# Recurrent unit's end: fifth gate's gelu behind the last root, six early half outputs of the projection in four passes

## The chip, the core and the metric

The kernel runs on one core of one Trainium2 chip. The core has a matrix engine (TensorE, PE in the profile; PEld is its weight load), a vector engine (VectorE, DVE), a scalar engine that evaluates functions from loaded tables (ScalarE, ACT), GpSimd (POOL) and a queue engine that issues transfers (SyncE, SP). Each works through its own instructions in a fixed order; semaphores tie them together. Data lies in SBUF, 128 partitions wide, and matrix products go to PSUM, which has eight banks. The metric is the device time of one execution in microseconds (us).

## The reference, cut to what matters

One inference step of two layers over 640 tokens (512 latent, 128 context) of width 1024. Layer 0 is attention and a gated feed-forward network (FFN). Layer 1, where the change lies, is a recurrent unit and another FFN:

```python
gate, xr = split(xm @ w_in)                       # two halves, 1024 wide each
xc = centred_depthwise_conv(xr)                   # width 4
r, i = sigmoid(xc @ w_a + b_a), sigmoid(xc @ w_i + b_i)   # 8 blocks of 128, per direction
a = exp(log_a);  log_a = -8 * r * softplus(-lam)
b = sqrt(-expm1(2 * log_a)) * (i * xc)            # "the root"
h_t = a_t * h_{t-1} + b_t                         # one scan per direction
y = (h_forward + h_backward) * gelu(gate)
x = x + g1 * (y @ w_out)                          # "the projection"
x = x + g2 * swiglu(modulate(rms_norm(x)))        # the FFN
```

## The kernel before, in words

All activations are kept with features on the partitions: 1024 features are KT = 8 tiles of 128, numbered 0 to 7, and the 640 tokens run along the free side. Products are in full precision by splitting: each operand is a rounded `hi` and a remainder `lo`, and a tile of a product is three matmuls, hi*hi, hi*lo and lo*hi (`some`, L227 to L229). A weight block `unit` (L163) is loaded to `raw` (three buffers), rounded to `hi` (in the recurrent unit by a transfer on POOL's queue, L178, elsewhere by ACT, L180) and its remainder is made by DVE (L182). `whi` and `wlo` have three buffers each; in the last stage every second block takes a second set, `whx` and `wlx`.

**The recurrent unit** is a pipeline over the eight feature tiles, in the loop at L1458. At step t the program writes down: block t's convolution and gate matmuls with their Tanh (`lru_a`), tile t+1's product xr (`lru_xr`), block t-1's Exp, Tanh and root (`lru_b`, the root is the Sqrt at L1305), block t-2's two scans (`lru_c`, L1316, and their sum, L1323 and L1324), the gelu gate of tile t-2 (`lru_gate`) and its output (`lru_d`): y times gelu (L1328, DVE), then the split of y into `yhi` (L1333, ACT) and `ylo` (L1335, DVE). Gates 1 to 7 are thus written at steps 3 to 9.

Gelu, Exp with Tanh, and Sqrt lie in different tables of ACT. `turn` (L1266) chains the functions in the order of the program and writes a table load (L1270) where the table changes. In the steady state a step has three loads: Exp, Sqrt and Gelu. A gate has two halves in PSUM, 384 and 256 tokens: the first is copied out at once (L1343), the second stays in its bank until gelu reads it there (L1346), and then gelu runs over the copied part.

PSUM in this stage: three banks `mm` (for xr, the gates and, later, the projection), one `at`, and two pairs `gp` for the gate matmuls of `lru_a`. When the last of these is read, the four banks become `mx` (three) and `mc` (one) of the next stage.

**The projection** (`project_halves`, L1028) makes 8 outputs in two halves of 320 tokens, CH = (0, 320), (320, 640). Of the half outputs a few are `early`: they are begun over the input tiles 0 to 5 of y while the recurrent unit is still finishing, in `mm` and `mx` banks in turn, and closed over tiles 6 and 7 in a second pass, with four matmuls on constants in between (`keep`, L206) that hold the clock up. There are five: both halves of outputs 0 and 1, and the first half of output 2. Then follow the first halves of outputs 3 to 7, and then the second halves of outputs 2 to 7 (DEH = 6). `out` adds the result to x (`residual`, L597) and stores it; x itself is loaded back from DRAM first (`load_x`, L1355), into memory that the recurrent unit's buffers held. `stat` sums the squares (L550, L553), and the normalisation of the first token half (`first_half`: L994, L995, L1333, L1335) is written between the second halves, two tiles at a time. The FFN's first products (`plain`, L1154) read it.

The order on each engine is not the program's: a planner simulates a timeline with its own costs when the program is built, takes the instructions in the order of the program where several are ready, and places others earlier where an engine would wait. So matmuls of the projection come between those of the last gates. `issue_after` and `pin` force an order where they stand.

Of the kernel before, what the change touches and what calls it, by code (L numbers as in the profile page):

```python
# [17 lines left out]
KT = D // P  # L18
# [3 lines left out]
CH = ((0, 320), (320, 640))  # L22
# [20 lines left out]
DEH = 6  # L43
# [82 lines left out]
class _Step:  # L126
# [901 lines left out]
    def project_halves(self, w, hi, lo, gk, key, xd):  # L1028
        def out(f, t0, t1, ps):
            self.residual(f, t0, t1, ps, G, True)  # L1030
            self.nc.sync.dma_start(xd[f * P:f * P + P, t0:t1], self.x[:, f, t0:t1])
        G = self.need(self.gcols, gk)
        us = [self.unit(w[f], "m") for f in range(3)]
        early = [(f, t0, t1) for f in range(3) for c, (t0, t1) in enumerate(CH) if c == 0 or f < KT - DEH]
        pss = [(self.ps("mx") if j % 2 else self.pg(False))[:, 0:HT] for j in range(len(early))]
        for ks in (range(KT - 2), range(KT - 2, KT)):
            if ks[0]:
                self.keep(self.ps("at"), 4)
            for (f, t0, t1), ps in zip(early, pss):
                self.some(us[f], hi, lo, t0, t1, ps, ks)  # L1040
                if ks[0]:
                    out(f, t0, t1, ps)
        for f in range(3, KT):
            us.append(self.unit(w[f], "mx"[f % 2]))
            out(f, *CH[0], self.chunk(us[f], hi, lo, *CH[0]))
        self.rt = self.t([P, NTOK], F32, "r", 2)
        for c, (t0, t1) in enumerate(CH):
            for f in range(KT - DEH, KT) if c else ():
                out(f, t0, t1, self.chunk(us[f], hi, lo, t0, t1))
                j = f - KT + DEH  # L1050
                for k in range(max(0, 2 * j - 2), 2 * j) if f < KT - 1 else ():
                    self.first_half(k, key)
            self.stat(t0, t1)
            self.nc.scalar.copy(self.rt[:, t0:t1], self.r[0][:, 0:t1 - t0])
# [302 lines left out]
    def run(self):  # L1357
# [82 lines left out]
        yhi = self.big()  # L1440
        ylo = self.big()
        with self.phase("lru", at=1) as lp:
            A, B, C, G = {}, {}, {}, {}
            self.table, self.last_act = AF.Gelu_apprx_tanh, None
            self.xrs = [self.t([P, 648], F32, f"xr{j}", 1, lp) for j in range(2)]
            for xr in self.xrs:
                for a, b in ((0, 2), (514, 517), (645, 648)):
                    nc.gpsimd.memset(xr[:, a:b], 0.0)

            def gate(g, after=None):  # L1450
                G[g], halves = self.lru_gate(g, xhi, xlo, lp, after)
                return halves
            x0, g0, x1 = self.lru_xr(0, xhi, xlo), gate(0, self.sq), self.lru_xr(1, xhi, xlo, self.dg)
            x0[0](pins={3: self.at})
            g0[0](pins={0: self.rr})
            for step in (x1[0], x0[1], g0[1]):
                step()
            for t in range(KT + 2):  # L1458
                if t < KT:
                    A[t] = self.lru_a(t, lp)  # L1460
                if t + 1 < KT:
                    for step in self.lru_xr(t + 1, xhi, xlo) if t else x1[1:]:
                        step()
                if 0 < t <= KT:
                    B[t - 1] = self.lru_b(t - 1, *A.pop(t - 1))
                if t > 1:
                    C[t - 2] = self.lru_c(t - 2, *B.pop(t - 2))
                if t > 2:
                    for step in gate(t - 2):
                        step()  # L1470
                if t > 1:
                    self.lru_d(t - 2, C.pop(t - 2), G.pop(t - 2), yhi, ylo)
            nc.gpsimd.dma_start(o["nh"], self.st)
        x1, x2 = self.big(n=NTOK + 2), self.big(n=NTOK + 2)
        self.new_x(self.ctx)
# [32 lines left out]
```

## Time and profile before

| | |
|---|---|
| median of 3 runs | 1519.43 us (1516.95 to 1521.25) |
| the profiled execution | 1518.63 us, of which the span of instructions is 1516.9 us |
| granted clock of TensorE, mean | 0.996 of full speed |
| recurrent unit, projection | about 840 to 1020 us, then until about 1066 us |
| last root (L1305) starts | 1008.66 us |
| last remainder of y (L1335) ends | 1021.35 us |
| transfers in all | 196.65 MB, 130 GB/s |

The page gives the busy time of each engine; a busy PE is not PE at its peak. A row of a timeline is: start in us, duration in us, engine, line, operation, output<-input by the program's names, count, and in brackets the idle time of the engine before it and what ended it. A row of waits is: who waited for whom, us in total, times, the longest. Rows by stage give busy times with counts of instructions in brackets.

### The profile page before, as it was taken

To read this page: it belongs to the slowest core of one execution; us is meant where nothing else is said; L and a number is where in the kernel's file an instruction comes from. 1 tells how busy PE (TensorE), PEld (TensorE's weight loads), DVE (VectorE), ACT (ScalarE), POOL (GpSimd) and SP (SyncE) were. 2 spreads that over 40 slices of the span, in tenths; PEclk is the share of its full clock that TensorE was granted. 3 is DMA by queue.
4 is the path that set the end of the run, shared out by engine and by line. 5 is a ranking of instruction groups with operands and counts; after the bars stand their busy time and mean duration, and the time that the engine had idled before them with its cause. 6 is when DMAs were issued, how large, how long until landed. Compare 5 with 4: busy or idle time off the path is not lost. (4 is left out here: it accounts for less than half of the span.)

```text
span 1516.9 us, 26173 instructions
## 1 busy us (share of the span) xinstructions
PE 1490.0 (98%) x10397; PEld 1443.2 (95%) x10397; DVE 1063.5 (70%) x2005; ACT 702.6 (46%) x1270; POOL 260.6 (17%) x276
## 2 busy tenths in 40 slices
PE   8999999999999999999999999989999999999997
PEld 6999999899999999999999988889999999999997
DVE  5778998679999997434443768886975665566555
ACT  4676766654332123312321568884644342434243
POOL 0112132101111110000000014230332323222211
PEclk9999999999999999999999999999999999999999
DMA  9544665446566664222222544325242231323211
GB/s 376 175 142 159 187 190 168 118 141 193 180 182 196 206 197 132 62 84 84 65 69 87 153 133 128 105 68 198 70 152 84 70 112 56 104 64 98 70 57 70
DMA packets 72330, 196.65 MB, mean 130 GB/s; under 512 B 8048, under 2 KB 24592, under 8 KB 72080
## 3 DMA queue, kind: packets, MB, share of 16 engines
q1 hardware_dynamic: 57392, 142.32, 29.7%
q0 software_dynamic: 14240, 51.98, 11.3%
q8 instruction: 81, 1.33, 0.4%
q10 hardware_dynamic: 576, 0.68, 0.1%
q14 instruction: 41, 0.34, 0.1%
HBM read 179.48 MB, written 8.92 MB: 124 GB/s over the span
## 5 line engine op out<-in xcount | busy, mean ns | idle before, releaser
L227 PE MATMUL mm<-big,whi 128*128 128x320 f32 (+3 forms) x1233 | 385.4, 314 | 5.7 <-ACT gl L1346 3.0
L228 PE MATMUL mm<-big,whi 128*128 128x320 f32 (+3 forms) x1233 | 384.8, 312 | 4.9 <-DVE big L1335 4.7
L229 PE MATMUL mm<-big,wlo 128*128 128x320 f32 (+3 forms) x1233 | 383.5, 312 | 0.0
L227 PEld LDWEIGHTS mm<-big,whi 128*128 128x128 f32 x1233 | 233.7, 190 | 8.6 <-ACT gl L1346 3.5
L228 PEld LDWEIGHTS mm<-big,whi 128*128 128x128 f32 x1233 | 234.1, 190 | 6.9 <-DVE big L1335 5.3
L229 PEld LDWEIGHTS mm<-big,wlo 128*128 128x128 f32 x1233 | 233.6, 190 | 1.0
L256 DVE SCALAR_TENSOR_TENSOR mprod<-mraw,csb 128x1024 f32<-128x1024 f32 x160 | 195.6, 1222 | 11.9 <-DMA mraw<-in_wm 11.4
L597 DVE SCALAR_TENSOR_TENSOR x<-mm,G,x 128x320 f32<-128x320 f32 (+2 forms) x192 | 78.0, 435 | 81.8 <-PE mm L229 81.5
L180 ACT CAST whi<-raw 128x1024 fp32r<-128x1024 f32 (+1 forms) x71 | 73.9, 1041 | 112.5 <-PE mm L228 65.5
L182 DVE TENSOR_TENSOR wlo<-raw,whi 128x1024 fp32r<-128x1024 f32 (+1 forms) x87 | 105.8, 1216 | 27.4 <-ACT whi L180 11.4
L227 PE MATMUL mm<-big,whx 128*128 128x320 f32 (+3 forms) x348 | 108.3, 311 | 0.0
L229 PE MATMUL mm<-big,wlx 128*128 128x320 f32 (+3 forms) x348 | 108.0, 310 | 0.0
L228 PE MATMUL mm<-big,whx 128*128 128x320 f32 (+3 forms) x348 | 107.8, 310 | 0.0
L252 POOL DMA_DIRECT2D mraw<-in_wm x80 | 43.1, 539 | 359.0 <-DVE mprod L256 266.1
L227 PE MATMUL mx<-big,whi 128*128 128x320 f32 (+3 forms) x287 | 89.1, 311 | 0.0
L229 PE MATMUL mx<-big,wlo 128*128 128x320 f32 (+3 forms) x287 | 88.8, 310 | 0.0
L228 PE MATMUL mx<-big,whi 128*128 128x320 f32 (+3 forms) x287 | 88.6, 309 | 0.0
L180 ACT CAST whx<-raw 128x1024 fp32r<-128x1024 f32 (+1 forms) x40 | 41.1, 1030 | 86.7 <-PE mm L228 47.6
L227 PE MATMUL mx<-big,whx 128*128 128x320 f32 (+3 forms) x260 | 80.6, 310 | 0.0
L229 PE MATMUL mx<-big,wlx 128*128 128x320 f32 (+3 forms) x260 | 80.5, 310 | 0.0
L228 PE MATMUL mx<-big,whx 128*128 128x320 f32 (+3 forms) x260 | 80.3, 309 | 0.0
L1333 ACT CAST whi<-raw 128x1024 fp32r<-128x1024 f32 (+1 forms) x41 | 41.3, 1008 | 70.8 <-PE mm L228 44.8
(349 smaller groups left out, 3727.8 us busy)
## 6 DMA issues: line engine op xcount, KB each, us to landing
raw<-in_gu SPq DMA_DIRECT2D x88, 512.0 KB, 3.5
mraw<-in_wm POOLq DMA_DIRECT2D x80, 512.0 KB, 4.0
raw<-in_dn SPq DMA_DIRECT2D x24, 512.0 KB, 3.6
sw<-in_wm SPq DMA_DIRECT2D x16, 512.0 KB, 10.5
raw<-in_wqk SPq DMA_DIRECT2D x16, 512.0 KB, 4.6
raw<-in_wi SPq DMA_DIRECT2D x16, 512.0 KB, 3.5
whi<-in_wi POOLq DMA_DIRECT2D x16, 512.0 KB, 4.0
raw<-in_dn SPq DMA_DIRECT2D x16, 448.0 KB, 3.3
```

The source lines that it names most:

```text
L180: nc.scalar.copy(hi, raw)
L182: nc.vector.tensor_tensor(lo, raw, hi.bitcast(F32), ALU.subtract)
L227: nc.tensor.matmul(ps, hi[:, k], xhi[:, k, s], start=(k == 0), stop=False)
L228: nc.tensor.matmul(ps, hi[:, k], xlo[:, k, s], start=False, stop=False)
L229: self.done = nc.tensor.matmul(ps, lo[:, k], xhi[:, k, s], start=False, stop=(k == last)).ins
L252: nc.gpsimd.dma_start(w, self.i["wm"][l * 6 + j - 2, f])
L256: nc.vector.scalar_tensor_tensor(prod, w, 1.0, self.csb[:, s], ALU.mult, ALU.mult, accum_out=out[:, s, f:f + 1])
L597: self.nc.vector.scalar_tensor_tensor(xs, ps[:, a - t0:b - t0], G[:, s, f:f + 1], xs, ALU.mult, ALU.add)
L1333: self.nc.scalar.copy(hi, v)
```

## The change

In the recurrent unit step 7 writes no gate and no output. Step 8 writes, behind block 7's root and block 6's scans, gate 5 and its output, then gate 6 and its output. Step 9 writes gate 7 and its output as before. In the order of ACT's functions the gelu of gate 5 thus stands behind the last root, with those of gates 6 and 7.

In the projection six half outputs are early, both halves of outputs 0, 1 and 2, so the third `mx` bank is used as well. They are taken in four passes over y's tiles: 0 to 4, then 5, then 6, then 7, with the four constant matmuls ahead of the last pass, which also hands out the results. The loop of second halves begins at output 3.

```diff
-        early = [(f, t0, t1) for f in range(3) for c, (t0, t1) in enumerate(CH) if c == 0 or f < KT - DEH]
+        early = [(f, t0, t1) for f in range(3) for t0, t1 in CH]
         pss = [(self.ps("mx") if j % 2 else self.pg(False))[:, 0:HT] for j in range(len(early))]
-        for ks in (range(KT - 2), range(KT - 2, KT)):
-            if ks[0]:
+        for ks in (range(KT - 3), (KT - 3,), (KT - 2,), (KT - 1,)):
+            if ks[-1] == KT - 1:
                 self.keep(self.ps("at"), 4)
             for (f, t0, t1), ps in zip(early, pss):
                 self.some(us[f], hi, lo, t0, t1, ps, ks)
-                if ks[0]:
+                if ks[-1] == KT - 1:
                     out(f, t0, t1, ps)
...
         for c, (t0, t1) in enumerate(CH):
-            for f in range(KT - DEH, KT) if c else ():
+            for f in range(max(3, KT - DEH), KT) if c else ():
                 out(f, t0, t1, self.chunk(us[f], hi, lo, t0, t1))
...
                     C[t - 2] = self.lru_c(t - 2, *B.pop(t - 2))
-                if t > 2:
-                    for step in gate(t - 2):
+                for g in {KT - 1: (), KT: (KT - 3, KT - 2)}.get(t, (t - 2,)):
+                    for step in gate(g) if g > 0 else ():
                         step()
-                if t > 1:
-                    self.lru_d(t - 2, C.pop(t - 2), G.pop(t - 2), yhi, ylo)
+                    if g >= 0:
+                        self.lru_d(g, C.pop(g), G.pop(g), yhi, ylo)
```

## The prediction

> **What bounds the kernel now.** I read the page, the 5 us stages, PE's waits around the recurrent unit's end, then the timelines of PE, ACT and DVE from 960 to 1070 us. The page's first rows:
>
> ```profile
> span 1516.9 us, 26173 instructions
> PE 1490.0 (98%) x10397; PEld 1443.2 (95%) x10397; DVE 1063.5 (70%) x2005; ACT 702.6 (46%) x1270; POOL 260.6 (17%) x276
> ```
>
> TensorE (PE) sets the time, so an edit is worth the PE time that is lost where it acts. The rows of stages (columns: us, PE busy, PEld, DVE, ACT, POOL, granted clock, DMA share, GB/s) find such a place at the unit's end, and PE's waits there name two releasers:
>
> ```profile
> 1000.00:1010.00 10.00, 6.23 (x42) 5.46 (x40) 8.80 (x13) 9.88 (x13) 4.12 (x2) 1.00 0.18 53
> 1010.00:1013.00 3.00, 1.33 (x6) 1.31 (x6) 2.97 (x3) 2.72 (x5) 0.00 (x0) 0.50 0.00 0
> ```
>
> ```profile
> PE mm L228 <- DVE big L1335: 3.4, 1, 3.4
> PE mm L227 <- ACT gl L1346: 1.7, 1, 1.7
> ```
>
> ACT is busy 9.88 of 10 us, PE 6.23, and then the clock is at half. PE's timeline gives the price:
>
> ```profile
> 1002.02 0.31 PE L227 MATMUL mm<-big,whi 128*128 128x320 f32 x1
> ...
> 1008.87 0.42 PE L228 MATMUL mm<-big,whi 128*128 128x320 f32 x1 [3.37 <-DVE big L1335]
> ...
> 1009.72 0.31 PE L229 MATMUL mx<-big,wlo 128*128 128x320 f32 x1
> 1011.69 0.64 PE L227 MATMUL mm<-big,whi 128*128 128x320 f32 x1 [1.67 <-ACT gl L1346]
> ...
> 1016.65 0.35 PE L227 MATMUL mm<-big,whi 128*128 128x320 f32 x1
> ...
> 1019.37 1.05 PE L210 MATMUL at<-ident,ones 128*128 128x128 f32 x8
> 1020.18 0.39 PE L227 MATMUL mm<-big,whi 128*128 128x320 f32 x1
> ...
> 1024.72 0.31 PE L227 MATMUL mx<-big,whx 128*128 128x320 f32 x1
> ...
> 1039.00 0.31 PE L227 MATMUL mm<-big,whx 128*128 128x320 f32 x1
> ...
> 1042.54 0.31 PE L227 MATMUL mm<-big,whx 128*128 128x320 f32 x1
> ```
>
> A half output is eight input tiles of three matmuls: from 1039.00 to 1042.54, **3.54 us, or 0.443 a tile** ("fNcM" below is half M of output N). At half clock, from 1011.69 to 1016.65, six tiles took 4.96 us, 0.827 each: 2.30 lost. Of the five early halves, ten tiles in the mx banks lie before 1002.02; the other 30 need 13.29, and the four keep-warm matmuls 0.81 (1019.37 to 1020.18). They take from 1002.02 to 1024.72, 22.70 us. So 8.6 us are lost, and no edit here can win more. Counted to the work that the new order has done by then (f2c1 too), before ends at 1024.72 + 3.54 = 1028.26.
>
> **The change, part by part.** *Gelu 5 behind the last root.* ACT's order at the end:
>
> ```profile
> 998.85 1.28 ACT L1270 ACT_TABLE_LOAD   x1
> 1000.14 0.39 ACT L1346 ACTIVATE gl<-mm 128x256 f32<-128x256 f32 x1
> ...
> 1000.96 1.28 ACT L1270 ACT_TABLE_LOAD   x1
> 1002.26 0.93 ACT L1303 ACTIVATE lt<-lt,l_sm 128x643 f32<-128x643 f32 x1
> 1003.09 1.04 ACT L180 CAST whi<-raw 128x1024 fp32r<-128x1024 f32 x1
> 1004.03 0.72 ACT L1333 CAST big<-lt 128x640 fp32r<-128x640 f32 x1
> 1004.65 0.92 ACT L1304 ACTIVATE lt<-lt,l_sp 128x643 f32<-128x643 f32 x1
> ...
> 1008.66 1.28 ACT L1305 ACTIVATE lt<-lt 128x1286 f32<-128x1286 f32 x1
> 1009.96 1.28 ACT L1270 ACT_TABLE_LOAD   x1
> 1011.25 0.39 ACT L1346 ACTIVATE gl<-mm 128x256 f32<-128x256 f32 x1
> ...
> 1011.95 0.38 ACT L1346 ACTIVATE gl<-mm 128x256 f32<-128x256 f32 x1
> ```
>
> Root 6 ends just ahead of the load of 998.85. One table load now goes (1.29) and gelu 5's pair moves back (0.82): the first Exp of block 7 starts 2.12 earlier, where the load of 998.85 ends. The cast of y(5) at 1004.03 (0.62 to the next start) moves back too. So the last root starts at 1008.66 - 2.12 - 0.62 = 1005.92, 2.74 earlier; the three gelus follow a load, 0.70 apart, and free their mm banks at about 8.51 + 0.39 = **1008.9**, 1009.6 and 1010.3. The moved gate's weight transfers pass POOL's state copies and SP's loads in program order; they stay covered, since the last of them on POOL was issued some 40 us before:
>
> ```profile
> 970.25 0.53 POOL L178 DMA_DIRECT2D whi<-in_wi  x1 [8.70 <-PE mm L229]
> ```
>
> *The price of it.* Gate 5's second half keeps one of three mm banks until 1008.9 instead of 1000.5; gates 6 and 7 keep the others. So f0c0, f1c0 and f2c0, all in mm, cannot begin before 1008.9, where f0c0 had five tiles in from 1002.02. On DVE, y(5) = y*G now waits for gelu 5, and behind it stand y(6), the last scans, and y(7).
>
> *The sixth half* f2c1 takes the third mx bank, so three mx halves of five tiles can run without gelu: 15 tiles instead of 10 + 5, the same fill, if f2's weights are there. Those follow gate 7's second half (one of three whi buffers): cast at 1003.09, remainder by DVE:
>
> ```profile
> 1001.82 0.82 DVE L1328 TENSOR_TENSOR lt<-lt,gl 128x640 f32<-128x640 f32 x1
> 1002.55 1.28 DVE L1316 TENSOR_TENSOR_SCAN lt<-lt,cols,lt 128x512 f32<-128x512 f32 x1
> ...
> 1005.56 1.20 DVE L182 TENSOR_TENSOR wlo<-raw,whi 128x1024 fp32r<-128x1024 f32 x1
> ...
> 1009.97 1.50 DVE L1306 SCALAR_TENSOR_TENSOR lt<-lt,lt 128x1286 f32<-128x1286 f32 x1 [1.16 <-ACT lt L1305]
> ...
> 1012.92 0.82 DVE L1328 TENSOR_TENSOR lt<-lt,gl 128x640 f32<-128x640 f32 x1
> 1013.66 1.28 DVE L1316 TENSOR_TENSOR_SCAN lt<-lt,cols,lt 128x512 f32<-128x512 f32 x1
> ...
> 1018.90 0.83 DVE L1328 TENSOR_TENSOR lt<-lt,gl 128x640 f32<-128x640 f32 x1
> 1020.52 0.83 DVE L1335 TENSOR_TENSOR big<-lt,big 128x640 fp32r<-128x640 f32 x1 [0.79 <-ACT big L1333]
> ```
>
> y(5)'s product (0.73 to the next start) leaves the place ahead of the scans, so the remainder ends at 1005.56 + 1.20 - 0.73 = 1006.03. PE idles from 1002.02 to there, 4.0 us but for two matmuls; the third of f2c1's first tile waits, and all of PE behind it. Bounds: at full clock f2c1 is done at 1008.24 and hidden, PE goes on at 1008.95 with 33 tiles (14.62) and 0.81, and ends at 1024.38: **3.88 won**. At half clock, as before had it after waits of 3.37 and 1.67 us, for the same 4.96 us: f2c1 until 1010.16, one more slow tile (0.38), end at 1010.16 + 14.62 + 0.38 + 0.81 = 1025.97: **2.29 won**. I take this end, as it is nearest to the row that shows the clock fall.
>
> The rule that speaks against the change is in the Trainium skill, "TensorE: Matmul & The Clock Gate", Part 1 (The HAM clock gate): the clock halves after an idle window of about 3.4 us and returns after as long a busy one, the windows running freely. One gap of 4.0 us would by it be throttled more surely than waits of 3.37 and 1.67; the trace agrees so far that the matmuls between these two (1008.87 to 1009.72) still ran at full clock. With 3.4 us of half speed from 1006.03 the estimate by that page ends at 1025.3, 3.0 won.
>
> *Four passes.* Tile 5 is asked after 15 mm tiles, at 1008.95 + 6.65 = 1015.6 at the earliest. The last root ends at 1007.2; DVE's two products behind it take 2.95 (in before 1009.97 to 1012.92, ahead of y(6)), so at 0.74 each y(5) and y(6) are multiplied by 1011.7 and the last scans start there. y(7)'s product starts 5.24 behind the scans' start in before (1013.66 to 1018.90), now 0.74 more for y(5)'s remainder: at 1017.6, 1.3 earlier, and y(7)'s remainder ends 2.45 later, at 1020.1. PE asks for it at 1021.7 at the earliest (the end less six tiles): covered by 1.6; without that cover each us late costs one. If y(5)'s remainder lies ahead of that of y(6), between the scans and their sums, it is there by 1015.6 too: I cost it at nothing.
>
> *Outputs.* All six banks are now full when f3 starts, so it needs a residual add, and that needs x reloaded:
>
> ```profile
> 1019.88 2.18 SPq L1355 DMA_DIRECT2D x<-xd  x4
> DMA to landing us min/median/max: 3.9/5.9/8.5
> ```
>
> The reload follows y(7)'s product by 0.98: issue at 1018.6, landed 3.9 later at 1022.5, and the first banks are free about 1.2 later. f3 starts at 1024.4 to 1026.0: hidden, by 0.7 to 2.3; a reload that is later by more than that costs what is over.
>
> *One chunk less in the second half-loop* shortens what covers the normalisation of the first half:
>
> ```profile
> 1064.34 0.89 DVE L1335 TENSOR_TENSOR big<-x,big 128x320 fp32r<-128x320 f32 x2
> ...
> 1068.97 0.31 PE L1154 MATMUL mm<-big,whx 128*128 128x320 f32 x1
> ```
>
> From f7c0's end (1042.54) the last split took until 1065.23, 22.7; PE asked for it at 1068.97, 26.4 after. Now it asks 3.54 sooner, 22.9 after. Margin 0.2: I cost it at nothing.
>
> **Sum.** Profiled execution 1518.63 (span 1516.9 and 1.7 around it), less 2.29: 1516.34. It lies 0.80 under the median of 1519.43, so the median is forecast at **1517.1**, 0.15% under: within 0.3% (4.6 us), about what a measurement of this kernel can tell from no change.
>
> **Rivals.** *Full clock in the gap*: 3.88 won, median 1515.5. For it: the matmuls of 1008.87 ran full behind a gap; against: the 0.50 soon after.
>
> *The sixth half doesn't fill the gap*: a planner fixed PE's order; if it puts f2c1 behind f0c0, PE stands from 1002.02 to 1008.95, then 38 tiles (16.83), 0.81 and a half-clock loss of 2.30: 1028.89, 0.6 worse than before, median 1520.1. For it: the cast at 1003.09 sits in ACT's bound chain, and may slip behind the last root. Against: mx ran ahead of mm in the order of before.
>
> *Slower: the normalisation of the first half loses its cover.* If one step of that chain (its spread matmul, in PE's planned order) comes one chunk later, it lasts over 22.9 us: PE stands 3.54 - 0.2 = 3.3, and a gap of that size brings the half clock, 2.30. Less the 2.29 won: 3.3 slower, median 1522.7. For it: ACT and DVE work without a break in that chain; against: one chunk less of squares in it.
>
> **How the numbers follow.** Forecast 0.43, full clock 0.24, no filling 0.13, lost cover 0.13, and 0.07 for a replanned rest of either sign. Runs of before spread over 1516.95 to 1521.25, so 2 us are laid around each case: past -0.3% (under 1514.9) a third of full clock, an eighth of the forecast and half the rest, with some more for a first half better covered: 0.19. Past +0.3% (over 1524.0) a third of lost cover, a little of the others and half the rest: 0.10. Within: 0.71. The range runs from full clock less 3 to lost cover, 1512.5 to 1522.5.
>
> **What would show it.** Between the last two roots two table loads (Exp, Sqrt) in place of three; the last root at about 1005.9; mx matmuls near 1006 and mm from 1008.9; a clock row near 0.5 from 1006 to 1011; f3 at 1026.0; no new wait on x or on L1335 near 1065. Wrong, if PE's first mm matmul behind the gelus comes ahead of f2c1, if f3 waits on L597, or if PE waits over 1 us at L1154.

## The result, and the profile after

The changed kernel takes **1521.90 us** in the median of 13 runs (1519.96 to 1523.72), the kernel before 1519.39 in 13 runs beside them (1516.63 to 1521.84). The ratio is 1.0019, 95% interval [1.0011, 1.0027]: 2.5 us (1.7 to 4.1) slower, where 2.3 faster was forecast. It moved the other way than forecast. That it lies inside the range given and near the price of the slower rival (1522.7) is luck for the most part, as its parts are others than that rival's.

The profiled execution took 1523.25 us. First its rows of the span and of the busy time:

```profile
span 1521.4 us, 26168 instructions
PE 1492.0 (98%) x10397; PEld 1444.6 (95%) x10397; DVE 1061.9 (70%) x2005; ACT 700.7 (46%) x1269; POOL 261.7 (17%) x276
```

One table load of ACT is gone (1269 for 1270), the counts of the other rows are the same, and the span is 4.5 longer. Executions already differ before the changed place is reached: the root of block 4, far ahead of any changed instruction, starts at 964.40 in before and at 965.75 here, and between 962.73 and 966.08 in all fourteen profiles. The granted clock goes with it: without any stretch of half clock ahead of that root it starts at 962.73 to 962.87 (four profiles), with one of 3.41 us at 963.99 to 964.40 (five), with more at 965.18 to 966.08 (five). Instants of two profiles are therefore compared as distances from that root ("behind root 4" below). From it to the end of the span it is 552.5 us in before and 555.65 here, 3.15 more.

The rows by stage say where. Here are those of before and then those of after (columns: us, busy PE, PEld, DVE, ACT, POOL, granted clock, DMA share, GB/s):

```profile
1005.00:1010.00 5.00, 1.64 (x9) 1.14 (x8) 3.84 (x8) 4.92 (x6) 3.39 (x2) 0.99 0.36 105
1010.00:1015.00 5.00, 3.33 (x13) 3.31 (x13) 4.97 (x5) 3.45 (x6) 0.00 (x0) 0.50 0.00 0
1065.00:1075.00 10.00, 10.00 (x74) 9.85 (x73) 7.63 (x13) 5.25 (x8) 0.85 (x1) 1.00 0.49 175
```

```profile
1005.00:1010.00 5.00, 2.18 (x13) 1.93 (x13) 5.00 (x9) 4.92 (x5) 2.59 (x2) 1.00 0.35 105
1010.00:1015.00 5.00, 4.01 (x18) 4.01 (x19) 4.97 (x5) 4.17 (x9) 1.09 (x1) 0.70 0.00 0
1065.00:1075.00 10.00, 6.54 (x38) 6.30 (x37) 7.74 (x15) 4.41 (x9) 0.85 (x1) 0.83 0.43 141
```

The unit's end became a little better: more matmuls, and the clock at 0.70 in place of 0.50. The new loss is some 55 us later. There PE was full in before and now is busy 6.54 of 10, with a lower clock behind it. The waits of TensorE in after, from 985 to 1060 and from 1060 on (who waited for whom, us in total, times, longest):

```profile
PE mm L227 <- ACT gl L1346: 3.4, 1, 3.4
PE mx L229 <- DVE wlo L182: 0.7, 1, 0.7
PE mx L227 <- ACT whi L180: 0.6, 1, 0.6
```

```profile
PE at L550 <- DVE ssq L536: 3.5, 1, 3.5
...
PE mm L1154 <- ACT g L1162: 0.9, 1, 0.9
```

The wait at L550 is new. L550 sums the squares of the second token half, which DVE adds up at L536. TensorE's timeline in before:

```profile
1065.89 0.31 PE L1154 MATMUL mm<-big,whx 128*128 128x320 f32 x1
...
1069.41 0.38 PE L550 MATMUL at<-ones,ssq 128*128 128x128 f32 x2
...
1070.67 0.40 PE L1154 MATMUL mm<-big,whi 128*128 128x320 f32 x1
...
1072.06 0.31 PE L1154 MATMUL mm<-big,whi 128*128 128x320 f32 x1
```

and in after:

```profile
1065.63 0.31 PE L229 MATMUL mm<-big,wlx 128*128 128x320 f32 x1
1069.40 0.46 PE L550 MATMUL at<-ones,ssq 128*128 128x128 f32 x2 [3.46 <-DVE ssq L536]
...
1071.43 0.61 PE L1154 MATMUL mm<-big,whi 128*128 128x320 f32 x1
...
1073.72 0.31 PE L1154 MATMUL mm<-big,whi 128*128 128x320 f32 x1
...
1074.60 0.83 PE L567 MATMUL mx<-dg,ones 128*128 128x128 f32 x6
1075.19 0.39 PE L1154 MATMUL mx<-big,whx 128*128 128x320 f32 x1
```

In before the FFN's first product (weights `whx`, bank `mm`) runs from 1065.89 to 1069.41, 3.5 us of work that covers DVE's squares; the sums L550 then wait for nothing. In after that product is not there. TensorE goes from the last half output straight to L550, stands 3.46, and the first product comes at 1075.19, in an `mx` bank, behind the spread L567. The matmuls behind the gap are slow: from L550 to the second product's fourth tile 4.32 us (1069.40 to 1073.72) against 2.65 (1069.41 to 1072.06) for the same work in before, 1.67 more. 3.46 + 1.67 = 5.1 lost; the wait for `g` later is 0.5 shorter (0.9 for 1.4), which leaves 4.6.

At the unit's end the first matmul behind the six early halves starts at 1028.19, 62.44 behind root 4; without the sixth half's 3.54 that is 58.90, against 60.32 in before: **1.42 won**. 4.6 lost less 1.4 won is the 3.15 by which the profile is longer.

ACT's order at that place:

```profile
1000.20 1.28 ACT L1270 ACT_TABLE_LOAD   x1
...
1003.00 1.05 ACT L180 CAST whi<-raw 128x1024 fp32r<-128x1024 f32 x1 [0.58 <-PE mm L228]
...
1006.67 1.28 ACT L1270 ACT_TABLE_LOAD   x1
1007.97 1.28 ACT L1305 ACTIVATE lt<-lt 128x1286 f32<-128x1286 f32 x1
1009.26 1.28 ACT L1270 ACT_TABLE_LOAD   x1
1010.55 0.38 ACT L1346 ACTIVATE gl<-mm 128x256 f32<-128x256 f32 x1
```

### The profile page after: what moved, and what is told of

It is laid out like the page before. It is cut to its first block, busy times and chain, and to the rows that moved or that the text cites. A ratio compares the mean times of both kernels' runs of the same rounds, so it can differ in the third digit from the quotient of the medians.

```text
span 1521.4 us, 26168 instructions
## 1 busy us (share of the span) xinstructions
PE 1492.0 (98%) x10397; PEld 1444.6 (95%) x10397; DVE 1061.9 (70%) x2005; ACT 700.7 (46%) x1269; POOL 261.7 (17%) x276
## 4 chain that ended last, share of the span: by engine, by line
PE 93%; DVE 3%; ACT 2%; DMA 1%; issue 1%; SPq 0%; DVEq 0%; POOL 0%; ACTq 0%; POOLq 0%
PE mm L227 15%; PE mm L229 15%; PE mm L228 15%; PE mx L227 5%; PE mx L229 5%; PE mx L228 5%; PE mx L1097 3%; PE mx L1098 3%; PE mx L1099 3%; PE gp L1291 2%; PE op L932 2%; PE tp L849 2%; PE mc L1097 1%; PE mc L1099 1%; PE mc L1098 1%; PE mm L243 1%
## 5 line engine op out<-in xcount | busy, mean ns | idle before, releaser
L227 PE MATMUL mm<-big,whi 128*128 128x320 f32 (+3 forms) x1221 | 381.0, 314 | 7.1 <-ACT gl L1346 4.8
L228 PE MATMUL mm<-big,whi 128*128 128x320 f32 (+3 forms) x1221 | 380.6, 312 | 1.9 <-DVE big L1335 1.7
L229 PE MATMUL mm<-big,wlo 128*128 128x320 f32 (+3 forms) x1221 | 379.7, 312 | 0.0
L227 PEld LDWEIGHTS mm<-big,whi 128*128 128x128 f32 x1221 | 230.9, 190 | 9.7 <-ACT gl L1346 5.3
L228 PEld LDWEIGHTS mm<-big,whi 128*128 128x128 f32 x1221 | 231.6, 190 | 3.7 <-DVE big L1335 2.1
L229 PEld LDWEIGHTS mm<-big,wlo 128*128 128x128 f32 x1221 | 231.0, 189 | 1.0
L597 DVE SCALAR_TENSOR_TENSOR x<-mm,G,x 128x320 f32<-128x320 f32 (+2 forms) x192 | 78.0, 436 | 85.2 <-PE mm L229 85.2
L182 DVE TENSOR_TENSOR wlo<-raw,whi 128x1024 fp32r<-128x1024 f32 (+1 forms) x87 | 105.8, 1216 | 28.0 <-ACT whi L180 12.5
L227 PE MATMUL mm<-big,whx 128*128 128x320 f32 (+3 forms) x360 | 112.0, 311 | 0.0
L229 PE MATMUL mm<-big,wlx 128*128 128x320 f32 (+3 forms) x360 | 111.5, 310 | 0.0
L228 PE MATMUL mm<-big,whx 128*128 128x320 f32 (+3 forms) x360 | 111.4, 309 | 0.0
L227 PE MATMUL mx<-big,whi 128*128 128x320 f32 (+3 forms) x299 | 92.9, 311 | 0.6 <-ACT whi L180 0.6
L229 PE MATMUL mx<-big,wlo 128*128 128x320 f32 (+3 forms) x299 | 92.5, 309 | 0.7 <-DVE wlo L182 0.7
L228 PE MATMUL mx<-big,whi 128*128 128x320 f32 (+3 forms) x299 | 92.2, 308 | 0.0
L227 PE MATMUL mx<-big,whx 128*128 128x320 f32 (+3 forms) x248 | 77.1, 311 | 0.0
L229 PE MATMUL mx<-big,wlx 128*128 128x320 f32 (+3 forms) x248 | 76.9, 310 | 0.0
L228 PE MATMUL mx<-big,whx 128*128 128x320 f32 (+3 forms) x248 | 76.7, 309 | 0.0
```

What stands on the lines that cost most here:

```text
L182: nc.vector.tensor_tensor(lo, raw, hi.bitcast(F32), ALU.subtract)
L227: nc.tensor.matmul(ps, hi[:, k], xhi[:, k, s], start=(k == 0), stop=False)
L228: nc.tensor.matmul(ps, hi[:, k], xlo[:, k, s], start=False, stop=False)
L229: self.done = nc.tensor.matmul(ps, lo[:, k], xhi[:, k, s], start=False, stop=(k == last)).ins
L597: self.nc.vector.scalar_tensor_tensor(xs, ps[:, a - t0:b - t0], G[:, s, f:f + 1], xs, ALU.mult, ALU.add)
```

## The experiments

**Why the first product moved.** `pg` hands out banks by a counter: of five calls two get an `mx` bank, where these may be shared. Both kernels call it three times for the early halves; the sixth half takes an `mx` bank by name. But the loop of second halves is one output shorter and calls it once less. So every later caller takes its predecessor's turn, and the FFN's first product gets `mx` where it had `mm`. The `mx` turn lies behind that of the spread. The first two kernels test this, each with one line at the head of the FFN's half-loop (`ffn_halves`): after with the turn set back,

```diff
     def ffn_halves(self, l, key, xd):
+        self.ng += 1
```

> The changed kernel, with the turn of the banks counted one on ahead of the FFN, so that the FFN's first product takes an mm bank again as in the kernel before. Theory A (the turn): the sixth early half takes one turn out of the loop of second halves, the FFN's first product comes to lie in an mx bank, whose turn follows the bank of the second stat's spread, and so PE has nothing between the last output and the second stat, where it waited 3.46 us at L550 and then ran part of 4 us at half clock. Then here the wait at L550 is under 0.3 us, the clock row of 1065 to 1075 is 1.00, and the kernel is 4 to 5 us faster than the changed one: median 1517 to 1518, 1.5 to 2.5 faster than before. Theory B (the cover): there is one chunk less to cover the normalisation and the squares, so PE waits for them whatever bank is taken: the first product waits at L1154 instead, 2 us or more, and the kernel is not faster than before. Theory C (the unit's end): the 3.44 us wait for gelu and the half clock behind it are the loss: slower than before by 1 us or more.

and before with the turn set on as the change does it:

```diff
     def ffn_halves(self, l, key, xd):
+        self.ng -= 1
```

> The kernel before, with nothing but the turn of the banks set one back ahead of the FFN, so that its first product takes an mx bank. Theory A: the second stat comes ahead of the first product; its squares were there at about 1067.9 and the last output ended at 1065.9, so PE waits about 2 us at L550, with or without a drop of the clock behind it: 1.5 to 4 us slower than before. Theories B and C: the chunk is still there and the unit's end is as before: no difference over 0.5 us.

After with the turn set back took 1519.08 (before beside it 1518.48), ratio 1.0003 [0.9994, 1.0012]. Before with the turn set on took 1521.05, ratio **1.0018** [1.0009, 1.0027]: the turn alone makes the unchanged kernel as slow as the change did. Waits of TensorE from 985 to 1075 us, first in after with the turn set back, then in before with it set on:

```profile
PE mm L227 <- ACT gl L1347: 3.4, 1, 3.4
PE mx L567 <- DVE dg L559: 1.2, 1, 1.2
```

```profile
PE at L550 <- DVE ssq L536: 1.9, 1, 1.9
PE mx L567 <- DVE dg L559: 1.3, 1, 1.3
```

The stage behind that gap of 3.4 us, in after with the turn set back, has full clock:

```profile
1010.00:1015.00 5.00, 4.24 (x29) 4.24 (x30) 4.96 (x6) 3.94 (x9) 0.86 (x1) 1.00 0.00 0
```

The wait at L550 goes with the turn in one kernel and comes with it in the other. That shows the cause of the loss, though not of its whole size: in before the wait is 1.9, in the changed kernel 3.46 (the section on the prediction has the rest). But the first kernel did not become faster than before, as I had expected of it; something else eats what the unit's end wins. Two things are left: a second wait, at L567 for the diagonal `dg`, and the unit's end itself.

**The unit's end, part by part.** Five early halves and the moved gate, over four passes; and the moved gate by itself in the kernel before:

```diff
-        early = [(f, t0, t1) for f in range(3) for t0, t1 in CH]
+        early = [(f, t0, t1) for f in range(3) for c, (t0, t1) in enumerate(CH) if c == 0 or f < KT - DEH]
...
-            for f in range(max(3, KT - DEH), KT) if c else ():
+            for f in range(KT - DEH, KT) if c else ():
```

> The changed kernel with five early halves instead of six: the moved gate and the four passes stay, the loop of second halves begins at output 2 again, and with it the turn of the banks and the cover are as before. All theories: no wait over 1 us at L550. For the unit's end by itself: without the sixth half PE has only ten tiles in mx, stands from about 1002 to the first gelu at about 1009, 7 us, and then the 30 tiles with a half clock: output 3 starts 0.5 to 1.5 us later than before, and the kernel is that much slower. Rival: the sixth half does nothing, its place is filled anyway, and the kernel wins the 1.4 us that the changed one had won there.

```diff
-                if t > 2:
-                    for step in gate(t - 2):
+                for g in {KT - 1: (), KT: (KT - 3, KT - 2)}.get(t, (t - 2,)):
+                    for step in gate(g) if g > 0 else ():
                         step()
...
```

> The kernel before with the moved gate alone (two passes, five early halves). The last root comes about 2 us earlier, but PE stands until the gelus, as in the run with five halves, 6 to 7 us: 0.5 to 1.5 us slower than before. Rival: the earlier root alone is what pays, 1 to 2 us faster.

They took 1520.64, ratio 1.0009 [0.9999, 1.0018], and 1520.01, ratio 1.0008 [0.9999, 1.0018]. The wait for gelu is the same in both; these are the row of the second, and its stage behind the wait:

```profile
PE mm L227 <- ACT gl L1346: 7.5, 1, 7.5
```

```profile
1010.00:1015.00 5.00, 4.58 (x17) 4.59 (x18) 4.97 (x7) 3.61 (x8) 0.52 (x1) 0.50 0.00 0
```

The moved gate turns before's waits of 3.37 and 1.67 into one of 7.5, and the clock behind it is at 0.50. Both intervals still include no difference, at their lower ends; neither run shows a gain. The reverse, six early halves and four passes with the turn set back and the gate left where it was, is the eighth run below.

**Three attempts to mend the changed kernel.** The wait at L567 has a plain reading in DVE's timeline: three weight remainders (L182, 1.22 each) stand between the squares and L555. I pinned them behind `var` (L555) instead of the squares, with the turn set back:

```diff
-        us = [[self.unit(self.i["gu"][l, c * NF + f], None, self.sq if f else None) ...
+        us = [[self.unit(self.i["gu"][l, c * NF + f], None, self.var if f else None) ...
```

> The changed kernel with the turn set back, and with the weight remainders of the FFN's units 1 and 2 (three at L182, 3.4 us of DVE) ordered behind the second stat's variance (L555) instead of behind the last square. In the run with the turn alone, output 3 started 2.9 us earlier than before by its own marks (less the moved chunk), and 1.23 us of that was given back at L567, where PE waited for DVE. Theory A with this second part (the shorter loop leaves DVE's weight remainders in front of the second stat): the wait at L567 is gone, no wait over 0.3 us takes its place before 1080, and the kernel is about 1.2 us faster than with the turn alone, 1 to 2 us faster than before. Rival: the remainders are then late for the FFN's third product, PE waits at L1154 as long, and nothing is won.

It took 1519.56, ratio 1.0011 [1.0002, 1.0020], and the wait at L567 rose from 1.2 to 2.0. DVE's timeline of this kernel shows why:

```profile
1071.34 0.16 DVE L555 TENSOR_SCALAR var<-at 128x3 f32<-128x3 f32 x1 [1.76 <-PE at L553]
1071.42 1.22 DVE L182 TENSOR_TENSOR wlx<-raw,whx 128x1024 fp32r<-128x1024 f32 x1
...
1074.83 0.55 DVE L559 TENSOR_TENSOR dg<-ident,rs 128x384 f32<-128x384 f32 x1
```

L559 follows L555 by 0.96 us at the least (a step on POOL between them), and the planner filled this place with all three remainders, 3.4 us. The pin has to stand behind L559.

On top of that edit, twelve constant matmuls in the gap, with the `mx` halves ahead of the `mm` halves in the first pass:

```diff
-            for (f, t0, t1), ps in zip(early, pss):
+            for j in (1, 3, 5, 0, 2, 4) if ks[0] == 0 else range(6):
+                (f, t0, t1), ps = early[j], pss[j]
+                if ks[0] == 0 and j == 0:
+                    self.keep(self.ps("at"), 12)
```

> As the last, and with twelve of the constant matmuls (2.4 us) put on PE between the sixth half's fifth tile and the first half in mm, that is into the gap before the gelus, which was 3.43 us. If the half clock behind that gap is what differs between executions (0.70 in the stage of 1010 to 1015 in the changed kernel's profile, 1.00 with the turn set back), the clock is 1.00 there in this profile and the median falls by 0.5 to 1.5 us against the run without them. Rival: the gap is too short to matter on most executions: no difference, or up to 0.5 us slower if the constants end behind the gelu.

It took 1524.14, ratio 1.0040 [1.0027, 1.0053]. The gap did keep full clock, and the unit's end was 2.65 better than in before (57.67 behind root 4 for 60.32). The loss, some 6.5 us, lies behind the second spread, where TensorE waits 2.7 for `g` and 1.4 for another stage's copy, and the clock falls (0.66 from 1100 to 1110). Its planned order there is another one. Why the planner chose it I did not find, so this run says nothing of the gap's price.

And, in place of that, the weights of outputs 0 and 1 rounded by POOL's queue instead of ACT, to start the last root earlier:

```diff
-        us = [self.unit(w[f], "m") for f in range(3)]
+        us = [self.unit(w[f], "m", fetch=f < 2) for f in range(3)]
```

> As the run with the late remainders, and the rounded weights of outputs 0 and 1 of the projection come by a transfer on POOL's queue instead of two casts by ACT (0.94 each to the next start) in the stretch before the last roots. If ACT's chain (last root, table load, gelu) sets when PE goes on at 1010.8, that comes 1 to 2 us earlier and so does output 3: median 1 to 2 us under the run with the casts. Rival: the transfers land later than the casts ended, PE waits for the weights in the mx halves, and the gelus come no earlier: no gain or 1 us slower.

It took 1519.01, ratio 1.0007 [0.9998, 1.0015]. The last root did start 1.1 us earlier, but no time came of it: TensorE then waits for the third output's remainder for 2.5 us (L229, on DVE's L182).

**The gate left where it was.** After with the gate's hunk undone and the turn set back:

```diff
-                for g in {KT - 1: (), KT: (KT - 3, KT - 2)}.get(t, (t - 2,)):
-                    for step in gate(g) if g > 0 else ():
+                if t > 2:
+                    for step in gate(t - 2):
                         step()
...
     def ffn_halves(self, l, key, xd):
+        self.ng += 1
```

> Six early halves in four passes with the turn set back, but the gate not moved: gelu 5 stays between the last two roots. Theory: the last root comes 2.6 us later, the mm banks of gates 6 and 7 come free at about 1011.6 and 1012.3 as in the kernel before, but f0c0 runs ahead and the sixth half fills the rest of the gap, so that only f1c0 and f2c0 wait: output 3 starts within 1 us of where it starts with the gate moved, and the kernel is no slower than the one with the turn alone by more than 1 us. Rival: the earlier root is what pays: 2 us or more slower than that.

It took 1516.45 (before beside it 1517.79), ratio **0.9991** [0.9982, 0.9999]: faster than before. Its waits from 985 to 1075:

```profile
PE mm L227 <- ACT gl L1347: 1.3, 1, 1.3
PE mx L229 <- DVE wlo L182: 1.3, 1, 1.3
PE mx L567 <- DVE dg L559: 1.2, 1, 1.2
PE mm L227 <- DVE x L597: 1.0, 1, 1.0
```

The gap of 3.4 is now two waits of 1.3. Five tiles of the first half of output 0 stand ahead of them (1001.64 to 1003.86), the sixth half's tiles between them, and the clock stays up:

```profile
1010.00:1015.00 5.00, 3.68 (x26) 3.68 (x26) 4.96 (x6) 3.08 (x6) 0.00 (x0) 1.00 0.01 3
```

The first matmul behind the early halves starts 60.16 behind root 4, 56.62 without the sixth half: 3.70 won at the unit's end, where the change won 1.42. Then the remainders, pinned behind `dg` (L559); the two passes of before over the six halves on top of that; and, without either of these two edits, the kernel with the gate left but the turn as the sixth half shifts it:

```diff
-        us = [[self.unit(self.i["gu"][l, c * NF + f], None, self.sq if f else None) ...
+        us = [[self.unit(self.i["gu"][l, c * NF + f], None, self.dg if f else None) ...
```

> Six early halves, four passes, the bank's turn set back, the fifth gate not moved (as in the run called t8_early_no_gate, whose time was 0.9991 of before), and the units' weight remainders (L182) pinned behind the diagonal of the second statistic's spread, L559, in place of its squares. Theory A (the remainders stand in front of L555 and L559 and make the spread's product wait 1.22 us): the wait of L567 for L559 falls under 0.3 us, and the time is 1.0 to 1.3 us below that of t8, so about 1515.2 us or 0.9982 of before. Rival B (the wait only moves: the first products of the feed-forward part then wait for a remainder instead): L567 waits little, but the products of the first unit wait about 1 us for L182, and the time is that of t8 within 0.5 us, 0.9988 to 0.9994 of before.

```diff
-        for ks in (range(KT - 3), (KT - 3,), (KT - 2,), (KT - 1,)):
-            if ks[-1] == KT - 1:
+        for ks in (range(KT - 2), range(KT - 2, KT)):
+            if ks[0]:
```

> As t9, but with the two passes of before (inputs 0 to 5, then 6 and 7) over the six early halves in place of four passes (0 to 4, 5, 6, 7). Theory A (the four passes only order the same 96 products so that input 5 is asked for later): the gap in front of the mm banks is there in both, and the time is that of t9 within 0.7 us, the waits for gelu and for L182 in the unit's end together 1 to 3 us in both. Rival B (the four passes are what wins at the unit's end): in two passes TensorE waits for the low part of input 5 in the middle of the first pass, 1 us or more that t9 doesn't have, and the time is 1 to 2 us above t9's.

```diff
     def ffn_halves(self, l, key, xd):
-        self.ng += 1
```

> Six early halves and four passes with the fifth gate not moved, and the bank's turn left as the sixth half shifts it: the change without its moved gate. Theory A (the shifted turn costs about 2.6 us wherever it stands, as it did in the kernel before with only the turn shifted, 1.0018 of before): TensorE waits 2 to 3.5 us at L550 for the squares L536, and the time is about 2.5 us above that of t8, some 1519 us or 1.0005 to 1.0010 of before. Rival B (the turn costs only together with the moved gate): no wait over 1 us at L550 and a time within 0.7 us of t8's, 0.9988 to 0.9995 of before.

Beside 1518.71 of before, they took 1516.97, ratio 0.9987 [0.9978, 0.9996]; 1515.10, ratio **0.9978** [0.9968, 0.9987]; and 1520.78, ratio 1.0015 [1.0006, 1.0024]. Waits of the first and the third, from 985 to 1075:

```profile
PE mm L227 <- ACT gl L1347: 1.3, 1, 1.3
PE mx L229 <- DVE wlo L182: 1.3, 1, 1.3
PE mm L227 <- DVE x L597: 1.1, 1, 1.1
```

```profile
PE at L550 <- DVE ssq L536: 3.5, 1, 3.5
...
PE mx L567 <- DVE dg L559: 1.2, 1, 1.2
```

The stage that holds the third kernel's wait at L550 shows no fall of the clock:

```profile
1062.00:1070.00 8.00, 4.09 (x30) 3.59 (x28) 6.65 (x12) 2.64 (x6) 0.82 (x1) 1.00 0.36 107
```

With the remainders in the right place the wait at L567 is gone: from root 4 to the span's end it is 549.31 us, after 550.58 with the wait. The medians move by less than the intervals allow to tell. The two passes gain nothing and lose nothing in the profile (549.23 to the end; no wait at L567 either); by medians they look better, with intervals that overlap. The turn costs 3.5 at L550 here too, at full clock: 554.61 to the end, 4.0 more than with the turn set back. It doesn't need the moved gate. This is more than I expected of it (1519 us), because in before with the turn set on the squares came 1.9 late, and here 3.5.

Last, the moved gate put back on the kernel with the remainders behind L559 and four passes:

```diff
-                if t > 2:
-                    for step in gate(t - 2):
+                for g in {KT - 1: (), KT: (KT - 3, KT - 2)}.get(t, (t - 2,)):
+                    for step in gate(g) if g > 0 else ():
                         step()
...
```

> t9 (six early halves, four passes, the bank's turn set back, the remainders behind L559) with the fifth gate moved behind the last root again, and nothing else: the change itself with the two edits in the feed-forward part. Theory A (the moved gate spreads the waits of the unit's end as one gap of about 3.4 us in front of the mm banks, in place of two of 1.3, and in many executions the clock drops behind it): TensorE waits 3.2 to 3.6 us there for gelu, and the time is 1.0 to 2.5 us above t9's 0.9987 of before, that is 0.9993 to 1.0004. Rival B (the moved gate wins the 0.7 to 1.3 us by which the last root starts earlier): 0.9978 to 0.9986 of before, below t9.

It took 1517.43 (before 1518.58), ratio 0.9994 [0.9985, 1.0003]. Its wait for gelu is 3.4 again; its stage behind it:

```profile
1010.00:1015.00 5.00, 5.00 (x26) 5.00 (x25) 5.00 (x7) 2.50 (x5) 0.68 (x1) 0.66 0.00 0
```

These kernels by distances from root 4 in the profiled executions (won at the unit's end is 60.32 less the start of the first matmul behind the early halves, and less 3.54 where there are six; the rest is the difference to before's 552.5 that this leaves). Each value is that of one execution: before with the turn set on is the program of before up to the FFN, and still differs from it by 0.44 at the unit's end.

| kernel | gate moved | turn | won at the unit's end | lost behind it | ratio to before |
|---|---|---|---|---|---|
| the change | yes | shifted | 1.42 | 4.57 | 1.0019 |
| turn set back | yes | as before | 2.91 | 1.10 | 1.0003 |
| five early halves, four passes | yes, five halves | as before | -0.56 | 0.19 | 1.0009 |
| before, gate moved | yes, five halves | as before | -1.64 | -0.22 | 1.0008 |
| before, turn set on | no, five halves | shifted | 0.44 | 3.21 | 1.0018 |
| turn set back, gate left | no | as before | 3.70 | 1.78 | 0.9991 |
| the same, turn kept | no | shifted | 3.74 | 5.85 | 1.0015 |
| and remainders behind L559 | no | as before | 3.67 | 0.48 | 0.9987 |
| and two passes | no | as before | 3.76 | 0.49 | 0.9978 |
| remainders behind L559, gate moved | yes | as before | 1.43 | 0.16 | 0.9994 |

With six early halves the moved gate is worse at the unit's end by 0.8 us where the clock stays up and by 2.2 to 2.3 where it falls. By medians the two pairs that differ in it alone give 0.0012 and 0.0007 of the time, about 1 to 2 us, with intervals that overlap: likely, and not settled by them. The last kernel but one beats both kernels: about 3.3 us under before, 6 under the change.

## Why the prediction went wrong, point by point

**The step that failed** is "One chunk less in the second half-loop": "Margin 0.2: I cost it at nothing." It took the order of the work behind the shorter loop as given, and only asked whether the first product's inputs would be ready 3.54 us sooner. The shorter loop moved that product itself. I had not followed what the removed call does to the turn of the banks, though the counter stands in the code the change touches. The price is the second statistic's squares uncovered, 3.46, and slow matmuls behind it, 1.67. A smaller part of the same step is the shorter loop itself: it brings DVE's squares 1.5 us later, as the next point shows, which is part of the 3.46, and costs 1.2 us at L567 where the first product is in its old place.

**The slower rival** had the place and nearly the price (3.3 and 2.30 forecast), but another victim: the normalisation of the first half. Its rows in after show no wait: L1154's only wait is 0.9, for `g`, as in before. What lost its cover was the statistic of the second half. For the larger part that is because its cover went elsewhere: the turn alone, in before, makes a wait of 1.9. The other 1.5 us are a longer chain, and near to what the rival had in mind. DVE behind the last output, in before and in after:

```profile
1066.09 0.68 DVE L597 SCALAR_TENSOR_TENSOR x<-mx,G,x 128x192 f32<-128x192 f32 x2 [0.46 <-PE mx L229]
...
1067.39 0.49 DVE L536 TENSOR_TENSOR ssq<-ssq,sq 128x320 f32<-128x320 f32 x1 [0.22 <-ACT sq L534]
```

```profile
1065.97 0.68 DVE L597 SCALAR_TENSOR_TENSOR x<-mm,G,x 128x192 f32<-128x192 f32 x2 [0.44 <-PE mm L229]
...
1066.97 1.29 DVE L1335 TENSOR_TENSOR big<-x,big 128x320 fp32r<-128x320 f32 x3
1068.17 1.08 DVE L536 TENSOR_TENSOR ssq<-ssq,sq 128x320 f32<-128x320 f32 x2
```

Three remainders of the first half's normalisation (L1335), done ahead of this place in before, now stand between the last residual and the last two squares, which end 3.28 us behind the residual's start, where it was 1.79. No run takes this part by itself; it is read from the timelines. I gave that rival 0.13; the range, which was to run up to it, ends at 1522.5, 0.2 short of its 1522.7.

**Gelu 5 behind the last root: right, with one term too large.** Two loads stand between the last two roots, as forecast. The last root starts 42.22 behind root 4, where before had 44.26: 2.04 earlier, forecast 2.74. The difference is the cast of the third output's weights at 1003.00: it waits 0.58 for a `whi` buffer and stands inside ACT's chain, ahead of the root.

**The sixth half: the mechanism was half right.** It fills time that was lost, but sooner than forecast: its remainder is there 39.61 behind root 4 (1005.36), forecast 41.63, so it was finished at full clock by 1007.55. The gap is not in front of it but behind it: 3.44 us until the first `mm` bank, and about 1 us later half clock. Won 1.42 where 2.29 was forecast; at full clock, as in the kernel with the turn set back, 2.91, where the bound was 3.88. The banks' 0.70 of delay accounts for most of either difference.

**The price of the moved gate** was named ("f0c0, f1c0 and f2c0, all in mm, cannot begin before 1008.9") and then set against the new order as a whole, which seemed to win anyway. The parts were not costed one by one. The sixth half alone wins 3.7 with the gate unmoved, in part because the 6.8 us of half clock that before has from 1009.91 do not come; the moved gate takes 0.8 to 2.3 of it back, though it starts the last root 2 us earlier. At the unit's end the bank that gate 5 gives back early is worth more than the earlier root; by the medians this is likely, as said above.

**Four passes cost nothing: right**, and they win nothing: 3.67 and 3.76 with four and with two passes, and no wait for y's low parts at L1335 in after. **Outputs hidden: right** in after, no wait on L597; it is thin, as the margin of 0.7 to 2.3 said. Where the unit's end is 2 us quicker, L597 holds TensorE for 1.0 us.

**The rule of the clock** (the Trainium skill, "TensorE: Matmul & The Clock Gate", Part 1): by its estimate one gap is throttled for about 3.4 us. After's gap of 3.44 was, from 1011.95 for 3.41 us; a gap of 3.43 in the kernel with the turn set back was not. With windows that run freely, as the page has them, and an idle one needed, gaps of this length would almost never be throttled. The runs agree with the free windows, and not with the idle one: here a window in which TensorE was busy for up to 1.46 us was enough, and the measurement decides (the last section has it).

None of the three marks that were to show the forecast wrong came up: the `mm` halves did not run ahead of the sixth half, nothing waited on L597, and L1154 waited under 1 us. They watched the places that I had costed, and the loss was at one that I had not.

## What to carry to other kernels

Where a resource is handed out in turn, an edit that removes one request shifts every later one; follow the counter to the next critical place before costing the edit at nothing, and look at which work comes to stand between two dependent steps. Cost the parts of a change apart: here one part won 3.7 us at its place, another gave 0.8 to 2.3 of it back, and a side effect of the first cost 3 to 4. An earlier end of the bounding chain is worth little if it is bought by holding the buffers that the critical engine could fill in the meantime.

## What was not expected of the hardware

Gaps of TensorE of one length were followed by different clocks. Behind 3.43 and 3.44 us the stage from 1010 to 1015 showed 1.00 in one kernel and 0.70, 0.71 and 0.66 in three others; behind the 3.46 at L550 the matmuls slowed down in after (0.83 from 1065 to 1075), and in the kernel with the gate left and the turn kept, with the same wait, the stage had 1.00. Behind 7.5 us the clock was at 0.50. The price of the gap varies by 1.5 us (2.91 and 1.42 won at the unit's end by two kernels that are the same up to there), on top of the gap itself.

The traces show what decides it. In each profile the stretches of half clock begin and end on one grid of steps of 3.41 us, which lies elsewhere in each execution. What counts is how long TensorE was busy within one step of that grid, and not how long the gap was. Steps at the unit's end, first of after and then two of the kernel with the turn set back, whose gap is as long:

```profile
1008.54:1011.95 3.41, 0.96 (x6) 0.96 (x7) 3.38 (x4) 3.38 (x7) 2.55 (x1) 1.00 0.00 0
```

```profile
1005.66:1009.07 3.41, 1.67 (x12) 1.40 (x10) 3.41 (x6) 3.36 (x4) 1.89 (x2) 1.00 0.46 154
1009.07:1012.48 3.41, 1.72 (x12) 1.72 (x13) 3.38 (x5) 3.40 (x7) 1.79 (x1) 1.00 0.00 0
```

In after most of the gap lies in one step, with 0.96 us of work, and the next step has half the clock. In the other it is shared between two, with 1.67 and 1.72, and the clock stays. Of all steps at full clock behind 900 us in the fourteen profiles, those with up to 1.46 us of work were followed by half clock and those with 1.55 or more by full clock. So the 3.46 at L550 in the kernel with the turn kept did nothing (1.55 and 1.82 in its two steps), and the 2.0 at L567 in the kernel with the late remainders brought half clock (1.46). Near 290 us and in the first 25 us some steps with 1.7 to 2.7 us of work were followed by half clock too, so this limit is one of this part of the kernel.

From this an estimate: laid at every place of the grid, TensorE's timeline with the moved gate and six early halves has a step under the limit in about nine places of ten, the timeline with the gate left and two waits of 1.3 in none (2.06 us of work at the least). So the full clock of the kernel with the turn set back was luck, and a gate that is moved mostly costs the larger price.

A pin tells a planner where an instruction may not stand, and not where it will: the remainders, moved from in front of L555 to behind it, filled the 0.96 us that DVE waits there with 3.4 us of work, and made the wait that they were to remove 0.8 longer.
